# Eight k-tile pairs of each down stage in seven block products, three of them with differences formed by an accumulating transfer

## The chip, the cores and the metric

The kernel runs on one core of a Trainium2 chip. The metric is the device time in microseconds of one execution. The engines are named as in the profile: PE is TensorE's matmul, PEld its weight load, DVE is VectorE, ACT is ScalarE, POOL is GpSimd, SP is the engine that issues most of the transfers.

## The reference

A decoder trunk of two layers over 256 tokens of width 1024. Layer A has differential attention with a causal mask, layer B attention in blocks (one block of 256 here) with keys and values of its own; both attend to a fixed memory of 256 rows as well. Each layer ends in a squared-ReLU block of width 4096, and this is the part that the change concerns:

```python
x = x + jnp.concatenate([o_self, o_mem], axis=-1) @ w_out
x = x + _sq_relu_mlp(_rmsnorm(x, norm_mlp), w_up, w_down)

def _sq_relu_mlp(h, w_up, w_down):
    u = jax.nn.relu(h @ w_up)
    return (u * u) @ w_down
```

All data are float32. The down product has 256 tokens, 4096 inner columns (32 k-tiles of 128) and 1024 outputs.

## The kernel before

**Products in three passes.** Each float32 operand is split into a high part (a copy that rounds to the type float32r) and a low part (the value less the high part), and a product is three matmuls: high by high, low by high, high by low. For weights, `chunk` loads a piece of [128, 1024] into one of four `w` buffers, ACT makes the high part in one of six `wh` buffers and DVE the low part in one of six `wl` buffers (line 364).

**Stages.** Mixer A (projections, attention, output projection), up A and down A (`mlp`), mixer B, up B and down B with the final norm (`mlp_last`). In an up stage `mlp_up` (from line 818) goes over 16 blocks of two column tiles, and leaves u squared as high and low parts in eight large buffers B0 to B7, four k-tiles in each. Each large buffer comes free once the products of its tiles are done.

**The down stages.** `natural_down` goes over the k-tiles, two at a time: a pair j is the k-tiles 2j and 2j + 1. Its product is a 2 by 2 block matter: u has the blocks (k-tile, half of the tokens), the weights the blocks (k-tile, half of the outputs). The ordinary way takes eight block products of three matmuls with 512 columns. For the pairs in the list `FAST`, `fast_pair` takes seven, by Winograd's form of Strassen's method. It needs four sums and differences of the u blocks, formed in the up stage by `block_sums`, and four of the weight blocks. With W00, W01 the halves of the first tile and W10, W11 those of the second, `diff` forms on DVE (line 963), in the room's blocks 0 to 3 of 512 columns each: W01 - W00, then W11 less that, W11 - W01, and W10 less block 1. `split` (lines 955 and 956) makes high and low parts of the four kinds of weights: W00 alone, the second tile (1024 columns), the room's blocks 0 and 1, the room's blocks 2 and 3. So a fast pair takes four of the six `wh` and four of the six `wl` buffers. The sums of u are split at lines 982 and 983. The seven products go to four cells of the result and to four further banks, which `gather` joins when the last fast pair is done.

Before, `FAST` is one list for both layers, and the room is one buffer, `near`, which all fast pairs share; it also serves one chunk of the up stage.

In down A the pairs 0 to 11 go through `natural_down`, and the last eight k-tiles follow by halves of the outputs. In down B all 32 k-tiles do, and the products of the last six k-tiles are put at the end, cell by cell, among the final norm's steps.

**The order.** Nothing is issued in the order of the code. `Plan.add` records each step with the engine, an estimated duration, what it reads and writes, and a priority (its place in the code less a shift). `Plan.order` then simulates the engines and picks at each moment the step that is ready and has the lowest priority; buffers of the classes in `fifo` are handed out in the order in which the code names them. The shifts, one for each kind of step and layer, are the table `EARLY`. The engines work in the order so found, each in order: an instruction that waits holds up all behind it. Loads go out on SP's queue alone.

Of the kernel before, what the change touches and what calls it, by code (L numbers as in the profile page):

```python
# [14 lines left out]
OP = mybir.AluOpType  # L15
# [9 lines left out]
HELD = 6  # L25
FAST = (0, 2, 4, 6, 8, 9, 11)
CW = 1024
LEAD = 16
MN = 7
SUMS = -10  # L30
# [8 lines left out]
EARLY = {k + l: 0 for k in KINDS for l in "AB"}  # L39
EARLY.update(wA=40, wB=-21, memA=20, memB=31, natA=25, natB=64, statA=-80, statB=-115, ropeA=-90, ropeB=9, scoreA=-92,  # L40
             scoreB=-37, ptA=136, ptB=-40, pvA=-41, pvB=145, finA=158, finB=85, evacA=55, evacB=167, prepA=154,
             prepB=60, normA=120, normB=36)
LOOK = 100
# [22 lines left out]
class Plan:  # L66
# [3 lines left out]
    LAT = 200  # L70
    SAME = {"pe": 0, "act": 130, "dve": 130, "pool": 130, "dma": 0}

# [52 lines left out]
    def order(self):  # L125
        look = {"pe": 0, "act": LOOK, "dve": LOOK, "pool": 0, "dma": 0}
        ready = {e: [] for e in self.SAME}
# [105 lines left out]
def tile_hybrid(ctx: ExitStack, tc: tile.TileContext, x0, xa, xb, xc, memt, xnat, mnat, w0, wall, consts, fgain, out):  # L233
# [8 lines left out]
    for i in range(8):  # L242
        caps[f"B{i}"] = 1
    P = Plan(caps, ("acc", "w", "wh", "wl", "v") + tuple(f"B{i}" for i in range(8)))
    uid = [0]
# [5 lines left out]
    def buf(cls, shape, dt=F32, pool=None):  # L251
        pool = pool or ring
        return Buf(cls, lambda slot: pool.tile(shape, dt, name=name(cls), tag=f"{cls}{slot}", bufs=1))
# [75 lines left out]
    def dma(dst, src, nbytes, r=(), w=(), pri=None, rate=0, lag=1900):  # L329
        rate = rate or 340  # L330
        P.add(("dma", max(470, nbytes / rate), lambda: nc.sync.dma_start(dst(), src)), r, w, lag=lag, pri=pri)

# [554 lines left out]

    def block_sums():

        sums = {}  # L890
        for i, j in enumerate(FAST):
            if i < 2:
                b = ppx_buf()
                dst, keys = (lambda b=b: b.t), [b]
            elif i < 5:
                dst = lambda i=i: vb.rearrange("p a b e -> p (a b e)")[:, (i - 2) * 512:(i - 1) * 512]
                keys = [("vb", n, hf) for n in range(2) for hf in range(2)]
            elif i == 5:
                dst, keys = (lambda: mv.rearrange("p a b e -> p (a b e)")), [("mv", 0), ("mv", 1)]
            else:  # L900
                n = ("mk", "qm")[i - 6]
                dst, keys = (lambda n=n: {"mk": mkr, "qm": qmr}[n]), [(n, 0), (n, 1)]
            sums[j] = dst, keys + [("s", j)]
        st_["sums"] = sums
        return sums

    def sums_room():

        room = buf("near", [128, 2048])
        return lambda a, b: room.t[:, a:b], lambda a: [(room, a)]  # L910

    def natural_down(us, pss, upto, held, gather, room, rk, depth):

# [3 lines left out]


        cells = list(pss)
        more = [bank("acc") for _ in range(4)]  # L920
# [22 lines left out]
        def fast_pair(n, j):  # L943

            i = st_["i"]
            st_["i"] += 2
            w = [buf("w", [128, CW]) for _ in range(2)]
            h = [buf("wh", [128, CW], F32R) for _ in range(4)]
            l = [buf("wl", [128, CW], F32R) for _ in range(4)]
            for a in range(2):  # L950
                dma(lambda a=a: w[a].t, wall[i + a], 4 * 128 * CW, w=[(w[a], 0), (w[a], 1)])
            old, P.shift = P.shift, EARLY["w" + st_["layer"]]

# [11 lines left out]
            def wb(a, c):  # L965
                return lambda: w[a].t[:, c * 512:c * 512 + 512]
            wk = [(x, c) for x in w for c in range(2)]
            split(0, wb(0, 0), [wk[0]], 512)
            diff(0, wb(0, 1), wb(0, 0), wk[:2])
            split(1, lambda: w[1].t, wk[2:])  # L970
            diff(1, wb(1, 1), lambda: t(0), [wk[3]] + rk(0))
            split(2, lambda: t(0, 2), rk(0) + rk(1))
            diff(2, wb(1, 1), wb(0, 1), [wk[1], wk[3]])
            diff(3, wb(1, 0), lambda: t(1), [wk[2]] + rk(1))
# [17 lines left out]
            k0, k1 = ukeys(us, 2 * j), ukeys(us, 2 * j + 1)  # L992
            end = n == len(FAST) - 1
            for ps, a, ak, x, c, last in (
# [7 lines left out]
        for k in range(upto):  # L1002
            if k // 2 in FAST:
                ch.append(None)
                if k % 2:
                    fast_pair(FAST.index(k // 2), k // 2)
                continue
            ch.append(chunk())
            if k < held:
                for hf, c in cells:  # L1010
                    mm(k, hf, c)
        return mm, product, u_

    def mlp(st, done):
        us = mlp_up(st, block_sums())
        pss = {(hf, c): bank("t") for c in range(2) for hf in range(2)}
        ys = {(hf, c): buf("q" + "hl"[c], [128, 512]) for hf, c in pss}

        def gather(more):
# [10 lines left out]
            for (hf, c), y in ys.items():  # L1030
                P.add(("act", t_act(512, False, True), lambda y=y, hf=hf: nc.scalar.activation(
                    y.t, y.t, AF.Copy, scale=st.r[:, hf:hf + 1])), [y, st.key], [y])

        part = 24
        _, product, u_ = natural_down(us, pss, part, part, gather,
                                      *sums_room(), 4)
        for c in range(2):
# [26 lines left out]
    def mlp_last(st):  # L1064
# [8 lines left out]
        for hf, c in cells:  # L1073
# [9 lines left out]
            xs[hf, c] = x  # L1083
        us = mlp_up(st, block_sums())
        pss = {cell: bank("t") for cell in cells}
# [24 lines left out]
        held = 32 - HELD  # L1110
        mm = natural_down(us, pss, 32, held, gather, *sums_room(), 4)[0]
        x, ps, tail = xs[1, 1], pss[1, 1], bank("acc")
# [372 lines left out]
```

## Time and profile before

| | |
|---|---|
| median of three runs | 589.21 us (588.25 to 590.46) |
| profiled execution | 589.23 us |
| its span, first to last instruction | 587.3 us |
| DVE differences of line 963 (three groups of 28, 14 and 14) | 19.2, 9.6 and 9.6 us |
| bytes moved by transfers | 107.38 MB, mean 183 GB/s |

The profile is that of one execution. Its page gives the busy time of each engine, the costliest groups of instructions with the idle time before them, and the transfers. Views of the trace give more: the order of time of one engine, the busy time of each engine in any stretch of the span, and who waited for whom. A matmul's row is longer than the time from its start to the next one's start, since matmuls are pipelined; so is a DVE row, by a little. Costs are therefore read from start to start. A time in brackets at the end of a row is idle time of the engine ahead of it, with what ended it.

### The profile page before, as it was taken

Reading aid. Unit: us, or ns where it says so; the run is one execution under the profiler, and the core shown is the slowest. Engines: PE = TensorE matmul, PEld = TensorE weight load, DVE = VectorE, ACT = ScalarE, POOL = GpSimd, SP = SyncE. Lnnn points to the kernel's source line nnn. Section 1 sums busy time; section 2 is a strip of 40 time slices with the busy share of each in tenths; the row PEclk is TensorE's granted clock in tenths of the full one; section 3 lists DMA queues with packets and bytes.
Section 4 is the critical chain, followed back from the end, with each engine's and each line's share of the span. In section 5 each row is a group of like instructions: output and inputs, shape, how many; then the busy total and the mean of one; then the engine's idle time right before and its main releaser. Section 6 shows DMA issues by size and latency. Waiting matters only on the chain.

```text
span 587.3 us, 10340 instructions
## 1 busy us (share of the span) xinstructions
PE 577.8 (98%) x3786; PEld 511.1 (87%) x3786; DVE 480.5 (82%) x838; ACT 410.7 (70%) x787; POOL 63.8 (11%) x74
## 2 busy tenths in 40 slices
PE   8999999999999999999999999999999999999995
PEld 7787778999999988888888887889999999888884
DVE  6798998787676889998988688797866677998985
ACT  6677988677667676576776588776776676656632
POOL 0422030240000000000112222001300000000002
PEclk9999999999999999999999999999999999999999
DMA  8666456447655545657577633324755564555521
GB/s 284 210 227 219 155 171 225 133 155 219 200 193 191 169 145 197 234 169 251 174 244 239 205 121 124 126 75 143 247 192 205 182 185 139 194 201 210 193 98 72
DMA packets 30866, 107.38 MB, mean 183 GB/s; under 512 B 3424, under 2 KB 3680, under 8 KB 30816
## 3 DMA queue, kind: packets, MB, share of 16 engines
q1 hardware_dynamic: 30528, 106.21, 54.3%
q8 instruction: 29, 0.48, 0.3%
q10 hardware_dynamic: 288, 0.52, 0.2%
q14 instruction: 21, 0.17, 0.1%
HBM read 105.67 MB, written 1.05 MB: 182 GB/s over the span
## 4 chain that ended last, share of the span: by engine, by line
PE 90%; DMA 4%; ACT 2%; DVE 2%; issue 1%; SPq 0%; POOL 0%; DVEq 0%; ACTq 0%; POOLq 0%
PE acc L864 30%; PE t L932 19%; PE acc L523 17%; PE acc L804 8%; PE acc L932 7%; PE t L623 2%; PE t L661 2%; DMA w<-memt 2%; PE t L718 1%; PE t L594 1%; ACT wh L362 1%; DMA w<-wall 1%; DVE wl L364 1%; DMA xT<-xb 1%; PE t L523 1%
## 5 line engine op out<-in xcount | busy, mean ns | idle before, releaser
L364 DVE TENSOR_TENSOR wl<-w,wh 128x512 fp32r<-128x512 f32 (+1 forms) x226 | 209.8, 951 | 45.4 <-ACT wh L362 44.3
L362 ACT CAST wh<-w 128x512 fp32r<-128x512 f32 (+1 forms) x227 | 177.3, 812 | 90.3 <-PE acc L864 41.2
L864 PE MATMUL acc<-xn,wh 128*128 128x256 f32 x1024 | 127.6, 277 | 0.0
L864 PEld LDWEIGHTS acc<-xn,wh 128*128 128x128 f32 x1024 | 121.5, 188 | 0.0
L932 PE MATMUL t<-wh,B 128*128 128x512 f32 (+1 forms) x344 | 104.6, 386 | 0.0
L932 PEld LDWEIGHTS t<-wh,B 128*128 128x128 f32 x344 | 64.2, 188 | 13.1
L523 PE MATMUL acc<-wh,xn 128*128 128x512 f32 x220 | 72.9, 398 | 0.5 <-ACT wh L362 0.5
L864 PE MATMUL acc<-xn,wl 128*128 128x256 f32 x496 | 66.5, 276 | 0.0
L932 PE MATMUL t<-wl,B 128*128 128x512 f32 (+1 forms) x172 | 66.3, 386 | 0.0
L864 PEld LDWEIGHTS acc<-xn,wl 128*128 128x128 f32 x496 | 61.0, 188 | 0.0
L482 POOL TENSOR_TENSOR sqa<-sqa,sq 128x256 f32<-128x256 f32 x28 | 27.0, 963 | 250.7 <-ACT sq L481 247.8
L523 PEld LDWEIGHTS acc<-wh,xn 128*128 128x128 f32 x220 | 41.3, 188 | 11.2 <-issue 1.8
L804 PE MATMUL acc<-B,wh 128*128 128x256 f32 x256 | 50.0, 287 | 0.0
L523 PE MATMUL acc<-wl,xn 128*128 128x512 f32 x110 | 43.1, 392 | 0.3 <-DVE wl L364 0.2
L804 PEld LDWEIGHTS acc<-B,wh 128*128 128x128 f32 x256 | 40.7, 189 | 0.6 <-issue 0.5
L955 ACT CAST wh<-near 128x1024 fp32r<-128x1024 f32 x28 | 29.3, 1054 | 13.4 <-DVE near L963 6.5
L932 PEld LDWEIGHTS t<-wl,B 128*128 128x128 f32 x172 | 32.3, 188 | 6.6 <-DVE wl L364 0.2
L955 ACT CAST wh<-w 128x512 fp32r<-128x512 f32 (+1 forms) x28 | 23.4, 835 | 18.2 <-PE t L932 12.2
L804 PE MATMUL acc<-B,wl 128*128 128x256 f32 x128 | 35.7, 279 | 0.0
L956 DVE TENSOR_TENSOR wl<-near,wh 128x1024 fp32r<-128x1024 f32 x28 | 33.9, 1223 | 1.9 <-ACT wh L955 0.5
L570 POOL TENSOR_TENSOR ropet<-ropes,consts 128x256 f32<-128x256 f32 (+1 forms) x28 | 26.0, 950 | 76.2 <-ACT ropes L559 58.6
L956 DVE TENSOR_TENSOR wl<-w,wh 128x512 fp32r<-128x512 f32 (+1 forms) x28 | 26.4, 954 | 7.1 <-ACT wh L955 7.1
(238 smaller groups left out, 906.5 us busy)
## 6 DMA issues: line engine op xcount, KB each, us to landing
w<-wall SPq DMA_DIRECT2D x188, 512.0 KB, 3.9
w<-memt SPq DMA_DIRECT2D x4, 512.0 KB, 5.2
w<-wall SPq DMA_DIRECT2D x6, 256.0 KB, 5.0
B<-mnat SPq DMA_DIRECT2D x2, 512.0 KB, 7.2
w<-w SPq DMA_DIRECT2D x2, 256.0 KB, 3.5
xT<-xc SPq DMA_DIRECT2D x2, 256.0 KB, 5.5
consts<-consts SPq DMA_DIRECT2D x1, 256.5 KB, 6.0
xT<-xb SPq DMA_DIRECT2D x1, 256.0 KB, 4.6
```

Source lines behind the costliest of these rows:

```text
L362: P.add(("act", t_act(n), lambda sl=sl: nc.scalar.copy(h.t[:, sl], w.t[:, sl])), [(w, x) for x in q], [(h, x) for x in q])
L364: P.add(("dve", t_dve(n), lambda sl=sl: nc.vector.tensor_sub(l.t[:, sl], w.t[:, sl], h.t[:, sl].bitcast(F32))), [(w, x) for x in q] + [(h, ...
L482: P.add(("pool", t_pool(S), lambda: nc.gpsimd.tensor_tensor(self.acc.t, self.acc.t, sq.t, op=OP.add)), [sq, self.acc], [self.acc])
L523: nc.tensor.matmul(pss[hf].t[:, c0:c1], a(k)[:, ts], b.t[:, o + c0:o + c1], start=(k == 0 and i == 0), stop=(k == KT - 1 and i == 2))
L570: nc.gpsimd.tensor_tensor(t.t[:, 0:nh, e:e + 32], zs.t[:, 0:nh, 32 - e:64 - e], b(sin[:, e:e + 32]), op=OP.mult)
L623: nc.tensor.matmul(sp[hd].t[:, c], qk[a].t[r, qb * 128:(qb + 1) * 128], qk[b].t[r, S:S + c.stop - c.start], start=(qb == 0 and i == 0 and ...
L661: nc.tensor.transpose(ps.t[:, i * 128:(i + 1) * 128], p.t[:, j * 128:(j + 1) * 128], ident)
L804: nc.tensor.matmul(o, a.t[:, ws], x(k), start=(n == 0 and m % 2 == 0 and i == 0), stop=(n == KT - 1 and i == 2), skip_group_check=True)
L864: nc.tensor.matmul(ps.t[:, o], w.t[:, k * 128:(k + 1) * 128], xnt[:, k, x], skip_group_check=True, **flags)
L932: nc.tensor.matmul(ps.t[:, c0:c1], x, y, start=start and i == 0, stop=stop and i == 2, skip_group_check=True)
L955: P.add(("act", t_act(m), lambda: nc.scalar.copy(h[x].t[:, :m], src())), keys, [h[x]])
L956: P.add(("dve", t_dve(m), lambda: nc.vector.tensor_sub(l[x].t[:, :m], src(), h[x].t[:, :m].bitcast(F32))), keys + [h[x]], [l[x]], port=True)
```

## The change

The list of fast pairs becomes one for each layer, with eight pairs instead of seven. For three of them (`ADDED`: numbers 0 and 5 of A's list, pairs 0 and 9, and number 6 of B's list, pair 11) blocks 0 and 2 of the room, W01 - W00 and W11 - W01, aren't formed on DVE. A transfer loads the first weight tile into them, ACT negates them, and a transfer issued by POOL adds the second halves of both tiles. The room of each fast pair is named in `ROOMS`: -1 is `near`, a number is that large buffer. `near` joins the classes handed out in order, the planner has a new engine for the accumulating transfers (1000 ns, and 4700 ns until they land), and the table `EARLY` has new numbers.

```diff
-FAST = (0, 2, 4, 6, 8, 9, 11)
+FAST = {"A": (0, 2, 4, 6, 7, 9, 10, 11), "B": (0, 2, 4, 6, 7, 10, 11, 12)}
+ADDED = {"A": (0, 5), "B": (6,)}
+ROOMS = {"A": (-1, -1, -1, 0, 0, -1, 2, -1), "B": (-1, -1, -1, -1, -1, 3, 2, 0)}
...
-EARLY.update(wA=40, wB=-21, memA=20, memB=31, natA=25, natB=64, statA=-80, statB=-115, ropeA=-90, ropeB=9, scoreA=-92,
-             scoreB=-37, ptA=136, ptB=-40, pvA=-41, pvB=145, finA=158, finB=85, evacA=55, evacB=167, prepA=154,
-             prepB=60, normA=120, normB=36)
+EARLY.update(wA=31, wB=-10, memA=20, memB=42, natA=10, natB=64, statA=-98, statB=-92, ropeA=-110, ropeB=35, scoreA=-92,
+             scoreB=-26, ptA=117, ptB=-20, pvA=-17, pvB=118, finA=175, finB=153, evacA=86, evacB=204, prepA=211,
+             prepB=34, normA=110, normB=14)
...
-    P = Plan(caps, ("acc", "w", "wh", "wl", "v") + tuple(f"B{i}" for i in range(8)))
+    P = Plan(caps, ("acc", "w", "wh", "wl", "v", "near") + tuple(f"B{i}" for i in range(8)))
...
-    def sums_room():
+    def sums_room(layer):
-        room = buf("near", [128, 2048])
-        return lambda a, b: room.t[:, a:b], lambda a: [(room, a)]
+        near = buf("near", [128, 2048])
+        which = []
+        rooms = {-1: (lambda a, b: near.t[:, a:b], lambda a: [(near, a)])}
+        for i in ROOMS[layer]:
+            if i not in rooms:
+                r = big(i, [128, 2048])
+                rooms[i] = (lambda a, b, r=r: r.t[:, a:b], lambda a, r=r: [(r, a)])
+            which.append(rooms[i])
+        return which
...
         def fast_pair(n, j):
+            room, rk = rooms[n]
...
-            for a in range(2):
-                dma(lambda a=a: w[a].t, wall[i + a], 4 * 128 * CW, w=[(w[a], 0), (w[a], 1)])
...
+            added = n in ADDED[layer]
+            if added:
+                def both():
+                    return room(0, 2048).rearrange("p (a b n) -> p a b n", a=2, b=2)[:, :, 0]
+                bk = rk(0) + rk(2)
+                dma(both, wall[i].rearrange("p (a n) -> p a n", a=2), 4 * 128 * CW, w=bk)
+                P.add(("act", t_act(CW), lambda: nc.scalar.mul(both(), both(), -1.0)), bk, bk)
+                P.add(("sw", 1000, lambda: nc.gpsimd.dma_start(
+                    both(), wall[i:i + 2, :, 512:1024].rearrange("a p n -> p a n"), accum_op=OP.add)), bk, bk, lag=4700)
+            for a in range(2):
+                m = 512 if added and not a else CW
+                dma(lambda a=a, m=m: w[a].t[:, 0:m], wall[i + a, :, 0:m], 512 * m, w=[(w[a], 0), (w[a], 1)])
...
-            diff(0, wb(0, 1), wb(0, 0), wk[:2])
+            if not added:
+                diff(0, wb(0, 1), wb(0, 0), wk[:2])
             split(1, lambda: w[1].t, wk[2:])
             diff(1, wb(1, 1), lambda: t(0), [wk[3]] + rk(0))
             split(2, lambda: t(0, 2), rk(0) + rk(1))
-            diff(2, wb(1, 1), wb(0, 1), [wk[1], wk[3]])
+            if not added:
+                diff(2, wb(1, 1), wb(0, 1), [wk[1], wk[3]])
```

More of the change, by code (lines that the diff above doesn't have):

```diff
@@ L70 @@
     LAT = 200
-    SAME = {"pe": 0, "act": 130, "dve": 130, "pool": 130, "dma": 0}
+    SAME = {"pe": 0, "act": 130, "dve": 130, "pool": 130, "dma": 0, "sw": 0}
     def __init__(self, caps, fifo):
@@ L125, in order @@
     def order(self):
-        look = {"pe": 0, "act": LOOK, "dve": LOOK, "pool": 0, "dma": 0}
+        look = {"pe": 0, "act": LOOK, "dve": LOOK, "pool": 0, "dma": 0, "sw": 0}
         ready = {e: [] for e in self.SAME}
@@ L886, in up_chunk, with block_sums @@
                   [("xnh", j) for j in range(k, k + 4)] + [(wl, k // 4)], [ps] + [between] * bool(between))
-    def block_sums():
+    def block_sums(layer):
         sums = {}
-        for i, j in enumerate(FAST):
+        for i, j in enumerate(FAST[layer]):
             if i < 2:
@@ L905, in block_sums, with natural_down @@
         return sums
-    def sums_room():
-        room = buf("near", [128, 2048])
-        return lambda a, b: room.t[:, a:b], lambda a: [(room, a)]
-    def natural_down(us, pss, upto, held, gather, room, rk, depth):
+    def sums_room(layer):
[8 more added lines that the diff above has]
+        return which
+    def natural_down(layer, us, pss, upto, held, gather, rooms, depth):
+        fast = FAST[layer]
         cells = list(pss)
@@ L949, in fast_pair @@
             l = [buf("wl", [128, CW], F32R) for _ in range(4)]
-            for a in range(2):
-                dma(lambda a=a: w[a].t, wall[i + a], 4 * 128 * CW, w=[(w[a], 0), (w[a], 1)])
-            old, P.shift = P.shift, EARLY["w" + st_["layer"]]
             def split(x, src, keys, m=CW):
@@ L967, in fast_pair @@
             wk = [(x, c) for x in w for c in range(2)]
+            added = n in ADDED[layer]
[10 more added lines that the diff above has]
+                dma(lambda a=a, m=m: w[a].t[:, 0:m], wall[i + a, :, 0:m], 512 * m, w=[(w[a], 0), (w[a], 1)])
+            old, P.shift = P.shift, EARLY["w" + st_["layer"]]
             split(0, wb(0, 0), [wk[0]], 512)
-            diff(0, wb(0, 1), wb(0, 0), wk[:2])
+            if not added:
+                diff(0, wb(0, 1), wb(0, 0), wk[:2])
             split(1, lambda: w[1].t, wk[2:])
@@ L992, in fast_pair @@
             k0, k1 = ukeys(us, 2 * j), ukeys(us, 2 * j + 1)
-            end = n == len(FAST) - 1
+            end = n == len(fast) - 1
             for ps, a, ak, x, c, last in (
@@ L1002, in natural_down @@
         for k in range(upto):
-            if k // 2 in FAST:
+            if k // 2 in fast:
                 ch.append(None)
                 if k % 2:
-                    fast_pair(FAST.index(k // 2), k // 2)
+                    fast_pair(fast.index(k // 2), k // 2)
                 continue
@@ L1014, in mlp @@
     def mlp(st, done):
-        us = mlp_up(st, block_sums())
+        us = mlp_up(st, block_sums("A"))
         pss = {(hf, c): bank("t") for c in range(2) for hf in range(2)}
@@ L1034, in mlp @@
         part = 24
-        _, product, u_ = natural_down(us, pss, part, part, gather,
-                                      *sums_room(), 4)
+        _, product, u_ = natural_down("A", us, pss, part, part, gather, sums_room("A"), 4)
         for c in range(2):
@@ L1083, in mlp_last @@
             xs[hf, c] = x
-        us = mlp_up(st, block_sums())
+        us = mlp_up(st, block_sums("B"))
         pss = {cell: bank("t") for cell in cells}
@@ L1110, in mlp_last @@
         held = 32 - HELD
-        mm = natural_down(us, pss, 32, held, gather, *sums_room(), 4)[0]
+        mm = natural_down("B", us, pss, 32, held, gather, sums_room("B"), 4)[0]
         x, ps, tail = xs[1, 1], pss[1, 1], bank("acc")
```

## The prediction

> **What bounds the kernel now.** I read the head of the page first, then the table of busy time by stretches (which I cut where the lines of the kernel change), then the order of time of single engines inside the down stages, then the waits.
>
> ```profile
> span 587.3 us, 10340 instructions
> ...
> PE 577.8 (98%) x3786; PEld 511.1 (87%) x3786; DVE 480.5 (82%) x838; ACT 410.7 (70%) x787; POOL 63.8 (11%) x74
> ```
>
> TensorE is busy for all but 587.3 - 577.8 = 9.5 us. The table by stretches says where those 9.5 us are. Its columns: stretch, its length, then busy time and count of PE, weight loads, DVE, ACT, POOL, the granted clock, the DMA share, GB/s. The stretches are head, mixer A, up A, down A (three), mixer B and its projection (two), up B, down B (two), tail.
>
> ```profile
> 0.00:25.00 25.00, 22.72 (x114) 18.03 (x115) 17.09 (x34) 17.00 (x36) 6.75 (x12) 1.00 0.83 269
> 25.00:122.00 97.00, 96.81 (x627) 81.41 (x627) 86.02 (x208) 77.91 (x221) 18.53 (x19) 1.00 0.54 184
> 122.00:209.90 87.90, 87.90 (x774) 87.86 (x773) 64.18 (x91) 62.60 (x89) 6.58 (x7) 1.00 0.56 181
> 209.90:254.90 45.00, 45.00 (x199) 37.25 (x200) 41.96 (x51) 29.32 (x35) 0.00 (x0) 1.00 0.59 202
> 254.90:266.50 11.60, 11.60 (x53) 9.61 (x52) 11.60 (x14) 7.71 (x10) 0.00 (x0) 1.00 0.60 209
> 266.50:292.20 25.70, 25.60 (x117) 21.00 (x116) 23.04 (x38) 20.13 (x38) 2.69 (x3) 1.00 0.60 205
> 292.20:398.20 106.00, 106.00 (x659) 87.61 (x658) 89.07 (x192) 76.82 (x192) 16.82 (x20) 1.00 0.50 164
> ...
> 497.70:557.60 59.90, 59.90 (x265) 49.58 (x266) 56.45 (x67) 39.70 (x47) 0.00 (x0) 1.00 0.58 203
> 557.60:580.40 22.80, 22.77 (x118) 19.29 (x116) 16.84 (x34) 8.08 (x19) 5.03 (x7) 1.00 0.25 89
> 580.40:587.30 6.90, 0.00 (x0) 0.00 (x0) 2.82 (x11) 1.12 (x3) 0.00 (x0) 0.86 0.20 76
> ```
>
> Two things are to be seen. First, the idle time of TensorE is 2.28 us of head, 6.90 us of tail and a few tenths between: every stage is bound by TensorE, the down stages too, at a granted clock of 1.00. Second, DVE is the runner-up, and in the down stages a close one: in down A up to 266.5 it is busy for 41.96 + 11.60 = 53.56 of 56.60 us (3.04 idle), in down B up to 557.6 for 56.45 of 59.90 (3.45 idle). In the up stage it has 87.90 - 64.18 = 23.72 us to spare.
>
> **The gain: products that go.** A k-tile pair done the ordinary way is eight block products, a fast pair seven; each product is three 512-column matmuls. One product, in the order of time on TensorE:
>
> ```profile
> 213.27 0.62 PE L932 MATMUL acc<-wh,xn 128*128 128x512 f32 x2
> 213.72 0.39 PE L932 MATMUL acc<-wl,xn 128*128 128x512 f32 x1
> 213.95 0.62 PE L932 MATMUL acc<-wh,xn 128*128 128x512 f32 x2
> ```
>
> From start to start that is 213.95 - 213.27 = 0.68 us, 0.227 us a matmul (the 0.39 us of one row overlaps the next). An ordinary pair is 8 x 0.68 = 5.44 us, a fast one 7 x 0.68 = 4.76. The lists go from seven to eight fast pairs in each layer, so two products, six matmuls, leave: 2 x 0.68 = 1.36 us. Nothing is added on TensorE. This is the whole gain, 0.23%.
>
> **The price on DVE.** The step to step times of DVE come from its order of time:
>
> ```profile
> 225.72 0.68 DVE L963 TENSOR_TENSOR near<-w,near 128x512 f32<-128x512 f32 x1
> 226.32 1.29 DVE L983 TENSOR_TENSOR xn<-vb,xn 128x512 fp32r<-128x512 f32 x2
> 227.59 1.23 DVE L956 TENSOR_TENSOR wl<-near,wh 128x1024 fp32r<-128x1024 f32 x1
> 228.74 1.22 DVE L364 TENSOR_TENSOR wl<-w,wh 128x1024 fp32r<-128x1024 f32 x1
> 229.87 0.68 DVE L963 TENSOR_TENSOR near<-w 128x512 f32<-128x512 f32 x1
> ```
>
> A 512-wide step takes 226.32 - 225.72 = 0.60 us, a 1024-wide one 229.87 - 228.74 = 1.13, say 1.14. A fast pair has six of the narrow (four differences, the short split, the split of a block sum) and three of the wide: 3.60 + 3.42 = 7.02 us. An ordinary pair has two wide ones: 2.28. So a fast pair needs 7.02 us of DVE for 4.76 us of TensorE, an ordinary one 2.28 for 5.44; turn about they fit (9.30 in 10.20), in a row they don't. One more fast pair costs DVE 7.02 - 2.28 = 4.74 us in each layer. Where a transfer forms two of the differences, two narrow steps go: 1.20 us, twice in A (pairs 0 and 9), once in B (pair 11). Net: +2.34 us in A, +3.54 in B. The block sums of the eighth pair are four short DVE steps more in each up stage, which its 23.72 us hide.
>
> Is there room? In A, pair 0 is prepared before 209.9, where DVE has time anyhow, so of its 1.20 us nothing counts later. From 209.9 to 266.5: idle 3.04, less 4.74 - 1.20 = 3.54, less 0.68 by which TensorE is sooner: 1.18 us short. In B up to 557.6: 3.45 - 3.54 - 0.68 = 0.77 short. These are the upper bounds of a new stall, 1.95 us. Lower bound nothing, for two reasons. What idle time DVE has there is not lack of work ahead but full buffers:
>
> ```profile
> 251.73 1.23 DVE L956 TENSOR_TENSOR wl<-w,wh 128x1024 fp32r<-128x1024 f32 x1 [1.04 <-ACT wh L955]
> ```
>
> DVE waits for ACT's split. The next row, from ACT's order of time, shows that ACT had waited for a product to release the buffer:
>
> ```profile
> 250.64 1.05 ACT L955 CAST wh<-w 128x1024 fp32r<-128x1024 f32 x1 [2.05 <-PE t L932]
> ```
>
> The change gives the differences of pairs 6, 7 and 10 in layer A and of 10, 11 and 12 in layer B other rooms than the one that all share now (buffers whose u tiles have been used), so DVE can form them in such gaps instead of waiting for the one room. And in B the last fast pair is now pair 12, after which come three ordinary pairs; behind 557.6 DVE has 22.80 - 16.84 = 5.96 us to spare. I take nothing, since TensorE's record has no gap in these stages (45.00 of 45.00, 59.90 of 59.90) with pairs 8 and 9 already side by side, and keep 1.95 for the range.
>
> **ACT, POOL and the queues.** A fast pair has five splits on ACT instead of two, and each of the three transfers brings a negation of 1024 elements, by the row below about 1.05 us; ACT has 45.00 - 29.32 = 15.68 us to spare in the first stretch of down A alone, so nothing counts.
>
> ```profile
> L955 ACT CAST wh<-near 128x1024 fp32r<-128x1024 f32 x28 | 29.3, 1054 | 13.4 <-DVE near L963 6.5 <-PE acc L864 3.2 <-PE acc L932 2.5
> ...
> w<-wall SPq DMA_DIRECT2D x188, 512.0 KB, 3.9
> ...
> B<-mnat SPq DMA_DIRECT2D x2, 512.0 KB, 7.2
> ```
>
> (The last two rows: size of one, median us to landing.) Each added pair loads 512 KB into the room, loads 256 KB less into the first w buffer and adds 512 KB by an accumulating transfer from POOL: 0.77 MB, three times 2.3 MB of 107. With a DMA share of 0.59 there is room. The room's load is issued on SP's queue, in order: if the room isn't free, the weight loads behind it wait too. The rooms are long free by the plan (near since pair 4, B2 since pair 5), so I take nothing.
>
> The accumulating transfer itself is in no row of this trace. Bounds: 3.9 us, if it goes like a load, and 3 x 3.9 = 11.7, if it reads its target, writes it and runs alone at a third of the pace; 7.2 is the longest landing shown for its size. The plan reserves 1.0 + 4.7 = 5.7 us. I take about that: between 3.9 and 7.2 it costs nothing, because the chain (load 3.9, negation 1.05, transfer) can start whole pairs ahead.
>
> POOL and DVE are seen to slow each other:
>
> ```profile
> L482 POOL TENSOR_TENSOR sqa<-sqa,sq 128x256 f32<-128x256 f32 x28 | 27.0, 963 | 250.7 <-ACT sq L481 247.8
> ...
> L1151 POOL TENSOR_TENSOR ql<-ql,ropes 128x256 f32<-128x256 f32 x2 | 1.4, 737 | 2.7 <-ACT sq L1140 2.7
> ```
>
> The same sum of 128x256 takes 963 ns in the up stages and mixers, beside a busy DVE, and 737 behind 557.6, where DVE has idle time. A transfer that POOL issues might be held up likewise, by 963 / 737 = 1.3 times: 0.3 us on the plan's 1.0, which the lead hides. The Trainium skill, SBUF — State Buffer, "Who interferes with whom", speaks against such transfers from POOL: its descriptors need a port that DVE's two-port modes lock; it adds that a sum of two tensors takes only the read side and so should not stop them. By the first half the three transfers would be held as long as DVE is in such a mode, by the second not at all; nearly all of DVE's steps in the down stages are such sums, so the sum above stands either way. No row here shows descriptor writing beside DVE.
>
> **The retuned leads.** They reorder work in every stage, the mixers above all. What can be won: in 25.0 to 122.0 TensorE is idle for 0.19 us, in 292.2 to 398.2 for none, in the head 2.28. With the 0.1 of down A that is at most 2.6 us, and part of the head is the first load, which no lead shortens. What can be lost has no such bound in the trace; DVE's 86.02 of 97.00 and 89.07 of 106.00 say that a late rope or turn can be made up for only in part.
>
> ```profile
> PE acc L523 <- ACT wh L362: 0.5, 1, 0.5
> ```
>
> That is TensorE's longest wait for a split of weights (total, times, longest, in us). I take zero, from -2.6 to +3; the 3 is an estimate, six waits of that length.
>
> **Sum.** Against the profiled execution, 589.23 us with a span of 587.3 (1.93 us lie around it; the median of the three runs is 589.21, the same within 0.02): 589.23 - 1.36 = 587.87. **587.9 us.**
>
> **Rivals.**
> 1. DVE takes over in the down stages. For it: 7.02 against 4.76 us for a fast pair, three of them in a row (9, 10, 11 in A; 10, 11, 12 in B), six wl buffers of which a pair takes four. Against it: the rooms and the ordinary pairs behind. At the full 1.95 us: 589.8; at half 588.9.
> 2. The leads gain as well: 587.87 - 2.6 = 585.3 at best; about 586.3 if a good half of it comes.
> 3. Slower: the accumulating transfers land late. The place is the difference of block 1 in pairs 9 (A) and 11 (B), a DVE step that needs the sum. DVE works in order, so behind it stand the splits of the same pair and of the next ones, and TensorE waits for those. It decides from where the lateness passes what DVE can make up, about its 3 us of idle. At 11.7 us instead of the plan's 5.7 it is 6.0 late, less 3.0, in two places: 6.0 us, 593.9. Pair 0 is sheltered by the up stage. For it: no row bounds that transfer, and DVE is nearly full. Against it: the room is free whole pairs ahead. The page DMA: Bandwidth & Descriptors of the Trainium skill, "Anatomy of one DMA", fits 2.0 us + bytes / 436 GB/s for plain transfers of this kind; as an estimate that is 3.2 us for 512 KB, which would leave the sum as it is.
> 4. The leads open gaps in the mixers: up to +3, 590.9.
> 5. The change does less than it says, because TensorE was not the bound there: excluded as to counts (six matmuls go), and the full stretches leave little doubt that each is worth its 0.227 us.
>
> **How the numbers follow.** Forecast with small deviations (587.2 to 588.6): 0.52. Rival 1 (588.6 to 589.8): 0.18. Rival 2: 0.10. Rival 3: 0.11. Rival 4: 0.09. A half per cent, about what a measurement of this kernel tells from no change, is 2.95 us: faster is below 586.3, slower above 592.2. Faster: most of rival 2, 0.08. Slower: most of rival 3 and the end of rival 4 joined with 1, 0.12. Same: 0.80. The range reaches from 585.8 to 591.5: below it lies a third of rival 2, above it rival 3 and little else, some 0.15 in all.
>
> **What would show it.** Right: the matmul rows of line 932's successor number 738 instead of 744, TensorE's busy time falls by about 1.4 us, stretches of the down stages stay full, DVE is busy near 100% there. Rival 1: weight loads or matmuls in the down stages that wait for DVE's wl splits, a few tenths each, in pairs 7 and 10 to 12. Rival 3: a DVE step idle for microseconds with a DMA into near or B2 as its releaser. Rivals 2 and 4: the head's or the mixers' idle time of TensorE changes while the down stages do what they should. The prediction is wrong if the down stages save something other than 0.68 us each, or if the mixers move by more than the saving.

## The result, and the profile after

The changed kernel takes 592.32 us (median of seven runs), the kernel before 588.78 in the same job. One of the seven took 642.93 us at a granted clock of 0.85; without it the median is 592.0, slower by 3.3 us, and the ratio is 1.0058 [1.0045, 1.0071]. Run again in another job (e16) it took 591.62 against 588.88, 1.0043 [1.0028, 1.0059]. The forecast was 587.9 with a range up to 591.5.

The page of the changed kernel (its profiled execution took 593.29 us, the longest of the other six): its span, the counts, and the rows of the transfers that are new (size of one, median us from issue to landing).

```profile
span 591.2 us, 10374 instructions
...
PE 578.3 (98%) x3780; PEld 509.7 (86%) x3780; DVE 486.5 (82%) x852; ACT 417.6 (71%) x798; POOL 66.7 (11%) x77
...
near<-wall POOLq DMA_DIRECT2D x2, 512.0 KB, 9.5
B<-wall POOLq DMA_DIRECT2D x1, 512.0 KB, 7.8
```

Six matmuls are gone, 3786 to 3780, yet TensorE's busy time rose from 577.8 to 578.3 and its idle time from 9.5 to 591.2 - 578.3 = 12.9 us. Why the busy time rose the runs do not show. The adding transfers land 9.5 (median of 8.3 and 10.6) and 7.8 us after their issue; the plan had 5.7. TensorE's waits (total, times, longest) name what is new beside the 1.1 us at the start that both kernels have:

```profile
PE t L596 <- ACT B L742: 1.3, 1, 1.3
PE acc L525 <- DVE wl L366: 1.2, 3, 0.8
...
PE acc L525 <- ACT wh L364: 0.5, 1, 0.5
PE t L596 <- ACT o L764: 0.5, 1, 0.5
PE t L942 <- DVE xn L1006: 0.5, 1, 0.5
```

L596 lies in mixer A, L525 in the products of the mixers (the wait of 0.8 at the hand-over from down A to mixer B), L942 is the down stage. None was there before but those of L525, with 0.2 and 0.5. The wait of 1.3 was 0.4 in e15 and none of 0.2 or more in e16, which have the same mixer A, so it isn't a steady cost.

One measure served through all runs: the **length of layer B's block**, from the first matmul of up B to the last of down B, read from TensorE's order of time. The ends for the kernel before,

```profile
408.61 0.48 PE L864 MATMUL acc<-xn,wh 128*128 128x256 f32 x2
...
580.09 0.28 PE L932 MATMUL acc<-wl,B 128*128 128x256 f32 x1
```

and for the changed one:

```profile
411.84 0.48 PE L866 MATMUL acc<-xn,wh 128*128 128x256 f32 x2
...
583.79 0.28 PE L942 MATMUL acc<-wl,B 128*128 128x256 f32 x1
```

That is 171.5 before and 172.0 after: longer by 0.5, though one product fewer should make it 0.7 shorter. The same reading from the first matmul of down A to the first of up B, called the **middle** below, gives 198.8 and 200.4. Both are read from one execution of each kernel. B's block repeats to 0.1 us between kernels with the same number of pairs in B and no adding transfer in it. The middle doesn't: it is 198.5 to 199.1 in the kernel before and e5, e6, e8, e10, e11 and e12, which have seven pairs in A and not the new table, so differences of up to 0.6 us in it tell little.

### The profile page after: what moved, and what is told of

It reads as the page before. It is cut to its first block, busy times and chain, and to the rows that moved or that the text cites. A ratio compares the mean times of both kernels' runs of the same rounds, so it can differ in the third digit from the quotient of the medians.

```text
span 591.2 us, 10374 instructions
## 1 busy us (share of the span) xinstructions
PE 578.3 (98%) x3780; PEld 509.7 (86%) x3780; DVE 486.5 (82%) x852; ACT 417.6 (71%) x798; POOL 66.7 (11%) x77
## 4 chain that ended last, share of the span: by engine, by line
PE 88%; ACT 4%; DMA 3%; DVE 3%; issue 1%; SPq 0%; DVEq 0%; ACTq 0%
PE acc L866 30%; PE t L942 19%; PE acc L525 14%; PE acc L942 8%; PE acc L806 8%; PE t L625 3%; DMA w<-wall 2%; ACT wh L364 2%; PE t L720 1%; PE t L663 1%; DVE wl L366 1%; PE t L525 1%; DMA w<-memt 1%; PE t L596 1%; SPq L333 0%
## 5 line engine op out<-in xcount | busy, mean ns | idle before, releaser
L942 PE MATMUL t<-wh,B 128*128 128x512 f32 (+1 forms) x320 | 97.1, 385 | 0.0
L525 PE MATMUL acc<-wh,xn 128*128 128x512 f32 x220 | 73.5, 399 | 0.7 <-ACT wh L364 0.5
L942 PEld LDWEIGHTS t<-wh,B 128*128 128x128 f32 x320 | 59.7, 188 | 12.1
L942 PE MATMUL t<-wl,B 128*128 128x512 f32 (+1 forms) x160 | 61.7, 386 | 0.1
L525 PEld LDWEIGHTS acc<-wh,xn 128*128 128x128 f32 x220 | 41.3, 188 | 12.3 <-issue 2.1
L525 PE MATMUL acc<-wl,xn 128*128 128x512 f32 x110 | 43.2, 393 | 0.5 <-DVE wl L366 0.5
L942 PEld LDWEIGHTS t<-wl,B 128*128 128x128 f32 x160 | 30.0, 188 | 6.6 <-DVE wl L964 0.6
L572 POOL TENSOR_TENSOR ropet<-ropes,consts 128x256 f32<-128x256 f32 (+1 forms) x28 | 24.2, 885 | 69.3 <-ACT ropes L561 56.3
L644 ACT ACTIVATE B<-t,small 128x128 f32<-128x128 f32 (+1 forms) x64 | 27.1, 439 | 4.1 <-DVE small L636 3.1
L942 PE MATMUL acc<-wh,xn 128*128 128x512 f32 x96 | 29.5, 389 | 0.0
```

Source lines behind the costliest of these rows:

```text
L525: nc.tensor.matmul(pss[hf].t[:, c0:c1], a(k)[:, ts], b.t[:, o + c0:o + c1], start=(k == 0 and i == 0), stop=(k == KT - 1 and i == 2))
L572: nc.gpsimd.tensor_tensor(t.t[:, 0:nh, e:e + 32], zs.t[:, 0:nh, 32 - e:64 - e], b(sin[:, e:e + 32]), op=OP.mult)
L644: nc.scalar.activation(p[hd].t[:, c], sp[hd].t[:, c], AF.Exp, bias=nm[hd][:, qb:qb + 1], accum_out=ss[:, hd, qb:qb + 1])
L942: nc.tensor.matmul(ps.t[:, c0:c1], x, y, start=start and i == 0, stop=stop and i == 2, skip_group_check=True)
```

## The experiments

All times are medians, beside the kernel before in the same job. The ratios with their 95% intervals are worked out from the single runs and aren't the quotients of the two medians (e8: 0.9986 by the medians, 0.9999 in the table, with one run of 592.27 us among its twelve). "Old leads" and "new leads" are the two tables `EARLY` of the diff.

### Which half of the change costs: e1 to e4

e1 is the kernel before with the new leads; e2 the changed kernel with the old leads; e3 the changed kernel without transfers of differences; e4 the changed kernel with two leads taken back.

```diff
# e1: before              EARLY.update(new numbers)
# e2: changed             EARLY.update(old numbers)
# e3: changed
-ADDED = {"A": (0, 5), "B": (6,)}
+ADDED = {"A": (), "B": ()}
# e4: changed
-EARLY.update(wA=31, ... natA=10,
+EARLY.update(wA=40, ... natA=25,
```

> The kernel before with the new table of leads alone (seven pairs, no added transfers). Theory L (most of the loss is the new leads: they put a weight load between the two loads of mnat, and tighten the start of mixer B): the first matmul of up A comes about 1.7 us later than before, that of up B about 3.6 us later, down stages as before; time about 592.0, ratio 1.0055. Rival T (the loss is the eighth pairs with their transfers): 588.7, ratio 1.000.

> The changed kernel with the old table of leads (eight pairs, transfers, rooms). Theory L: up A and up B start as in the kernel before; the down stages give back 1.36 us of products and lose about 1.3 us to late weight loads beside the transfers: 588.8 plus or minus 0.7, ratio 1.000. Rival T: 591.5 or more, ratio 1.005.

> The changed kernel with all differences on DVE (eight pairs, rooms, new leads, no transfers). Theory A (the transfers delay the weight loads beside them): the stall of about 1.1 us near the end of down B goes, the one in down A stays or grows to 1.3 us because DVE has 2.4 us more to do there; against the changed kernel between -1.0 and +0.5: 591.3 to 592.8. Rival D (DVE is the bound in the down stages, and the transfers relieve it): both down stages stall by 1 to 2 us more: 594 or more.

> The changed kernel with two leads put back, wA=40 and natA=25, after which the loads of mnat go out one behind the other as before. Theory L: the wait of about 1.8 us in mixer A (at 58 us) goes, up A starts 1.7 us sooner, mixer B keeps its loss: 590.6, ratio 1.003. If the mnat loads do not matter: 592.3.

| | us | before | ratio | B's block | middle |
|---|---|---|---|---|---|
| e1 | 590.47 | 588.87 | 1.0029 [1.0020, 1.0039] | 171.5 | 200.1 |
| e2 | 590.14 | 588.87 | 1.0020 [1.0002, 1.0038] | 172.2 | 199.4 |
| e3 | 590.80 | 588.87 | 1.0036 [1.0022, 1.0049] | 170.8 | 201.7 |
| e4 | 591.00 | 588.87 | 1.0036 [1.0024, 1.0048] | 172.3 | 199.5 |

Both halves cost, where theory L and rival T each named one: e1 is 1.5 us below the 592.0 of theory L, e2 1.3 above its 588.8. The new leads alone make the kernel before 1.6 us slower. The pairs with the old leads are 1.3 slower, where 1.36 faster was worked out. Without transfers B's block falls to 170.8, by just the 0.7 that a product less is worth. The total is 1.9 us above the kernel before, where the changed kernel is 2.7 (e16) to 3.3 above it. The middle grew to 201.7 in its profiled execution (592.67 us, the longest of its eight runs), and TensorE has a new wait in down A, at 269.2 us:

```profile
PE t L942 <- DVE xn L1006: 0.9, 1, 0.9
```

With this list, and without transfers, DVE is late in layer A by 0.85 us. (L1006 is DVE's split of a sum of u.) The changed kernel, e15 and e16 have the same list with the transfers of pairs 0 and 9, and no wait in down A: there the transfers did relieve DVE. Two leads taken back (e4) change little against e16's 1.0043.

### The eighth pair by layer: e5 to e8

All with the old leads. e5 has seven pairs in A, and in B the eight of the change with their rooms but no transfer; e6 is e5 with pair 11's transfer; e7 has the change's eight pairs, rooms and two transfers in A, and the old seven in B; e8 has seven in both, and pair 11 of B formed by the transfer in a large buffer.

```diff
# e5: changed, old leads
+FAST = {"A": (0, 2, 4, 6, 8, 9, 11), "B": (0, 2, 4, 6, 7, 10, 11, 12)}
+ADDED = {"A": (), "B": ()}
# e6: e5 with             ADDED = {"A": (), "B": (6,)}
# e7: changed, old leads
+FAST = {"A": (0, 2, 4, 6, 7, 9, 10, 11), "B": (0, 2, 4, 6, 8, 9, 11)}
+ADDED = {"A": (0, 5), "B": ()}
# e8: changed, old leads
+FAST = {"A": (0, 2, 4, 6, 8, 9, 11), "B": (0, 2, 4, 6, 8, 9, 11)}
+ADDED = {"A": (), "B": (6,)}
```

> Eight pairs in layer B alone, all differences on DVE, old leads, the rooms of B as in the change; layer A as in the kernel before. Theory A (the late weight loads beside the transfer cost down B its gain): without the transfer the gain of 0.68 us stands, nothing waits near the end of down B: 588.2 against 588.9, ratio 0.999. Rival D (DVE is short there, by 0.77 us plus the 1.20 us that the transfer took off it): a stall of 1 to 2 us in pairs 10 to 12, 589.5 or more.

> As e5, but pair 11's two differences by the transfer as in the change. Theory A: ACT and DVE wait 2 to 4 us for the weight loads beside the transfer, TensorE about 1.2 us near 556 us: 589.4, 1.2 us more than e5. Rival D: faster than e5, because DVE has 1.20 us less to do.

> Eight pairs in layer A alone, with its two transfers, old leads; layer B as in the kernel before. Theory E (the last splits of down A come later, so the loads of the memory for mixer B and its first weights start later against TensorE): down A gains 0.68 less 0.44, then TensorE waits about 1.0 us near the start of mixer B; up B starts about 0.8 us later than before: 589.6. Without such a hand-over: 588.4.

> The kernel before with one thing more: the two differences of pair 11 of layer B by the transfer (seven pairs, old leads). Theory A: DVE has 1.20 us less to do and yet the weight loads beside the transfer land late, ACT waits for them 3 us or more; TensorE stalls by 0 to 1 us: 588.9 to 589.9. If the transfer cost nothing: 588.9 and no wait of ACT for weights over 2 us in down B.

| | us | before | ratio | B's block | middle |
|---|---|---|---|---|---|
| e5 | 587.72 | 588.70 | 0.9987 [0.9976, 0.9998] | 170.8 | 198.5 |
| e6 | 589.80 | 588.70 | 1.0031 [1.0019, 1.0044] | 172.3 | 199.0 |
| e7 | 588.42 | 588.70 | 0.9999 [0.9989, 1.0009] | 171.4 | 199.1 |
| e8 | 587.88 | 588.70 | 0.9999 [0.9983, 1.0014] | 171.5 | 198.7 |

e5 has the product's gain and nothing else. Its DVE and ACT, in the order of time where pair 11 is prepared (idle time before a row in brackets, with what ended it):

```profile
539.40 1.05 ACT L963 CAST wh<-w 128x1024 fp32r<-128x1024 f32 x1 [1.58 <-DMA w<-wall]
...
539.47 0.69 DVE L971 TENSOR_TENSOR B<-w,B 128x512 f32<-128x512 f32 x1 [0.15 <-DMA w<-wall]
```

The same two steps in e6, with the transfer:

```profile
541.47 1.06 ACT L963 CAST wh<-w 128x1024 fp32r<-128x1024 f32 x1 [3.69 <-DMA w<-wall]
...
541.54 0.69 DVE L971 TENSOR_TENSOR B<-w,B 128x512 f32<-128x512 f32 x1 [2.44 <-DMA w<-wall]
```

Both engines start 2 us later (2.7, counted from the first matmul of up B, at 408.05 us in e5 and 407.41 in e6), and the releaser is not the sum that the transfer forms, which landed at 540.53: it is `w`, an ordinary weight load on SP's queue, issued at 534.71 and landed at 541.45. In the changed kernel the same step of DVE waits 2.19 us for `w<-wall`. What that does further on is in the table by stretches (length, then busy time and count of PE, weight loads, DVE, ACT, POOL), of e5 first:

```profile
545.00:556.00 11.00, 11.00 (x50) 9.13 (x49) 11.00 (x15) 7.23 (x9) 0.00 (x0) 1.00 0.54 179
```

and of e6:

```profile
545.00:556.00 11.00, 10.08 (x44) 7.74 (x43) 10.96 (x16) 7.78 (x9) 0.00 (x0) 1.00 0.50 162
```

DVE is full in both. In e5 it keeps TensorE fed for 11.00 of 11.00 us; in e6, with the later start, it doesn't make up the time, and TensorE does 44 matmuls instead of 50. (The two stretches are shifted by 0.64 us against each other; B's block, 170.8 and 172.3, is not.) e8 has a transfer for pair 11 too, but only seven fast pairs, and TensorE has no wait in the stage:

```profile
545.00:556.00 11.00, 11.00 (x50) 9.12 (x49) 9.41 (x11) 7.62 (x9) 0.00 (x0) 1.00 0.65 222
```

DVE has 1.59 us of 11 left there. But e8 differs in a second way: its transfer lands at 539.93, over 5 us before DVE's first use of the sum at 545.36, and neither ACT nor DVE waits for a load between 530 and 552. So that a late load costs only where DVE has no idle time left is argued from these three runs, not shown.

### What of the transfer is late: e10 and e11

e10 is e6 with a plain transfer of the same bytes in place of the adding one, so that the addition is left out; e11 is e6 with pair 0 instead of pair 11 formed by a transfer, in the up stage.

```diff
# e10: e6 with
-    both(), wall[i:i + 2, :, 512:1024].rearrange("a p n -> p a n"), accum_op=OP.add)), bk, bk, lag=4700)
+    both(), wall[i:i + 2, :, 512:1024].rearrange("a p n -> p a n"))), bk, bk, lag=4700)
# e11: e6 with            ADDED = {"A": (), "B": (0,)}
```

> As e6, but the transfer of POOL's queue writes the second halves instead of adding them (so the differences of pair 11 are wrong in value; same bytes, same waits, same queue). Theory P (an adding packet holds an engine twice as long, 197 against some 95 ns, and so the weight loads behind it come late): its packets take about 95 ns, ACT waits under 2.5 us for the weight load instead of 3.7, TensorE does not stall: 588.0, near e5. Rival Q (the queue itself is the cost: whatever POOL issues goes ahead of SP's loads): 589.8, as e6.

> As e6, but the transfer serves pair 0 instead of pair 11, so it runs in the up stage, where DVE is idle for a quarter of the time. Theory A: weight loads beside it may be late, but DVE makes it up: 587.8, as e5. Rival R (a transfer of POOL costs its 2 us wherever it stands): 589.8.

e10: 587.95, before 588.74, 0.9990 [0.9979, 1.0001], B's block 170.8. e11: 588.09, 0.9989 [0.9979, 0.9999], B's block 170.8. Neither has the 1.5 us of e6's 172.3. In e11 the transfer lands even later after its issue (7.7 us in e6), and TensorE has no wait in layer B's block:

```profile
near<-wall POOLq DMA_DIRECT2D x1, 512.0 KB, 8.3
```

So it is the adding, at that place. e10 tells how much lateness is too much. The same step of ACT there:

```profile
540.86 1.05 ACT L963 CAST wh<-w 128x1024 fp32r<-128x1024 f32 x1 [2.89 <-DMA w<-wall]
```

Counted from up B's first matmul (408.21) that is 1.3 us later than in e5, where e6 is 2.7 later. DVE is as full as in e6 (10.96 of 11.00 us from 545 to 556), and TensorE doesn't wait: 1.3 us are still made up for, 2.7 are not. The 2.89 us are more than the 2.5 that the expectation allowed.

The single packets in the trace show where the time goes. Here they are counted by the microsecond in which they start, with their bytes and mean duration (SP's counts hold the packets of 4 B that end a load, 14 of the 27 in 536 in e6):

```
                    packets of POOL's queue            SP's queue, us 535 536 537 538 539 540
e6  adding   256 of 2048 B, 194 ns, 536.2 to 539.8                 59  27   0   6  81 173
e10 plain    128 of 4096 B, 193 ns, 536.4 to 538.9                 69  66   0  48 125 161
```

For the same 512 KB the adding transfer needs twice the packets, each half as large but taking the same time: 256 x 194 / 16 = 3.1 us on all sixteen DMA engines, against 128 x 193 / 16 = 1.5. (The expectation had it that the plain packets would be as many and half as long; the total is the same.) And while either is served, SP's queue all but stops (33 packets from 536 to 539 in e6, 114 in e10; in the changed kernel one from 541 to 543). The Trainium skill, Collectives: The Full Stack, "The bandwidth ceiling: the fold count and why AG ≠ RS ≠ AR", says of ReduceScatter, a collective whose transfers add, that it is slower because the add needs two source reads, which makes its rate about half. The trace agrees with the half (3.1 against 1.5 us).

The Trainium skill, DMA: Bandwidth & Descriptors, "Queues, rings and completion order", says that a DMA engine goes round robin between its queues, but drains a whole packet, typically 9 to 17 descriptors, from one before it switches. Its packet is not a packet of the profile. The profile counts these on POOL's queue, in e6 and in e10:

```profile
q0 software_dynamic: 272, 0.52, 0.5%
...
q0 software_dynamic: 144, 0.52, 0.3%
```

Spread evenly over sixteen engines these are 17 and 9 for each, with the one of 4 B that ends its share. If each share goes as one packet of the skill's kind, SP's loads stand still for the whole transfer, and the trace agrees with that: in 537 they had none in either run, though in e6 one had been issued at 534.71. Where such a packet ends the profile doesn't show, so this cause of the standstill is argued; the standstill is shown.

### The eighth pair of A without transfers, and two leads: e9 and e12

e9 has eight pairs in both layers, no transfers, old leads, and another list in A; e12 is the kernel before with two of the new leads.

```diff
# e9: e5 with
+FAST = {"A": (0, 1, 3, 5, 6, 8, 10, 11), "B": (0, 2, 4, 6, 7, 10, 11, 12)}
+ROOMS = {"A": (-1, -1, -1, -1, -1, 0, -1, -1), "B": (-1, -1, -1, -1, -1, 3, 2, 0)}
# e12: before
-EARLY.update(wA=40, ... natA=25,
+EARLY.update(wA=31, ... natA=10,
```

> Eight pairs in both layers with all differences on DVE: layer B as in e5, layer A with the list 0, 1, 3, 5, 6, 8, 10, 11 and one second room, old leads. Theory A (the gain was lost to the transfers and the leads, not to DVE): both stages shorter by 0.7 us, 587.5 to 588.0 against 588.8, ratio 0.998; a hand-over to mixer B that is late (theory E) takes up to 0.7 us of it back. Rival D (DVE cannot carry eight pairs): 590 or more.

> The kernel before with two leads of the new table, wA=31 and natA=10, which put a weight load between the two loads of mnat and move the rest of mixer A's order. Theory L: these two are most of what the new leads cost: 590.1, ratio 1.0022; a wait of TensorE for ACT at 58 us. If the other leads cost it (mixer B): 588.8.

e9: 588.45, before 588.74, 0.9992 [0.9981, 1.0004], B's block 170.8, middle 199.8. e12: 588.63, 1.0004 [0.9993, 1.0015]. The pair of B gains its 0.7 again; that of A gains nothing, without transfers too, and TensorE has no wait in down A: with this list DVE carries eight pairs. The two leads are harmless alone.

### The leads by layer, the transfer alone, the change again: e13 to e16

e13 and e14 are the kernel before with the new leads of layer A's names only, and of layer B's only; e15 is the changed kernel without pair 11's transfer (`ADDED["B"] = ()`); e16 is the changed kernel.

```diff
# e13: before             EARLY.update(all ...A names new, ...B names old)
# e14: before             EARLY.update(all ...B names new, ...A names old)
# e15: changed
-ADDED = {"A": (0, 5), "B": (6,)}
+ADDED = {"A": (0, 5), "B": ()}
```

> The kernel before with the new leads of layer A only. The new table cost 1.7 us, two of its entries (wA, natA) nothing. Theory LA (the order of mixer A as a whole, with the split pair of mnat loads, is the cost): 590.2. Theory LB (the order of mixer B is the cost): 588.8.

> The kernel before with the new leads of layer B only. Theory LA: 588.8. Theory LB: 590.2, up B starts about 1 us later against up A than before.

> The changed kernel, all of it, less the one transfer of pair 11 in layer B. Theory A: the 2.1 us that this transfer cost in e6 against e5 come back here too: 590.2, no stall near 559 us. If the losses are not additive: 591.5 or more.

> The changed kernel once more, beside e15: 592.3, ratio 1.006. Its wait for ACT in mixer A at 58 us, 1.8 us in its first profile and 0.5 us in e1 with the same order of loads, is expected between those.

| | us | before | ratio | B's block | middle |
|---|---|---|---|---|---|
| e13 | 589.16 | 588.88 | 1.0006 [0.9996, 1.0016] | 171.5 | 199.4 |
| e14 | 589.37 | 588.88 | 1.0018 [0.9999, 1.0037] | 171.5 | 199.6 |
| e15 | 589.98 | 588.88 | 1.0023 [1.0011, 1.0034] | 170.8 | 199.7 |
| e16 | 591.62 | 588.88 | 1.0043 [1.0028, 1.0059] | 172.1 | 200.3 |

Pair 11's transfer costs the changed kernel 591.62 - 589.98 = 1.6 us. Neither theory LA nor LB came, since neither layer's numbers alone reach 590.2 us or e1's 1.0029; those of B come nearer, but with an interval that touches 1 (one of e14's runs took 595.47 us). TensorE's waits in e1 don't point to one place either:

```profile
PE acc L523 <- ACT wh L362: 1.0, 1, 1.0
PE t L1056 <- DVE qh L1047: 0.6, 1, 0.6
PE t L594 <- ACT o L762: 0.5, 1, 0.5
PE acc L523 <- DVE wl L364: 0.4, 2, 0.2
```

The first and the last are near the start, at 7 to 10 us, where the kernel before has 0.5 and 0.2; the L594 is in mixer A and the L1056 at the end of down A. The wait at L1056 stands in e13 too (0.7 us) and not in e14, so it comes of layer A's numbers. Layer B's show otherwise: from the last matmul of down A to the first of up B takes 114.8 us in e14 and e1, 114.1 in e13 and the kernel before, with the same matmuls. So both halves of the table have a part, in these traces 0.6 to 0.7 us each. That the new table costs 1.6 us is shown; which entries do it stays open.

### Where A's pair loses its gain: e17 and e18

In e7 ACT's order of time at the hand-over from down A to mixer B has this, and TensorE's the second row:

```profile
283.17 1.71 ACT L380 ACTIVATE wh<-w,xT 128x256 fp32r<-128x256 f32 x4 [1.63 <-DMA w<-memt]
...
292.71 0.50 PE L525 MATMUL acc<-wl,wh 128*128 128x512 f32 x1 [0.73 <-DVE wl L366]
```

ACT stands still for the second load of layer B's memory rows. Behind it in its order are the normed input and the first weight splits of mixer B, and TensorE waits 0.73 us for the low part of one of those, which DVE forms behind ACT. That wait is 0.4 to 1.1 us in the seven runs so far with eight pairs in A other than e15, which has none, and in the runs with seven no such wait stands there. The load is later by more than the 0.68 us that the stage is shorter: counted from the first matmul of down A, it is issued after 65.6 us in all ten kernels with seven pairs in A and after 68.3 to 69.6 in all ten with eight. Why it is issued later the runs don't show. e17 and e18 are e9 and e7 with one edit: the planner expects layer B's memory loads 1.6 us later, and so gives ACT other work first.

```diff
-            dma(lambda w=w: w.t, memt[:, 4 * a:4 * a + 4], 4 * 128 * CW, w=[w])
+            dma(lambda w=w: w.t, memt[:, 4 * a:4 * a + 4], 4 * 128 * CW, w=[w], lag=1900 + 1600 * (st_["layer"] == "B"))
```

> Eight pairs in A and in B, the old leads, no transfer of differences (as e9, 588.45 at 0.9992), and the planner is told that layer B's memory loads land 1.6 us later than it thought. Theory: the eighth pair of A gives back its 0.68 at the hand-over to mixer B, because the second memory load lands after the time at which ScalarE's in-order stream asks for it (waits of 1.3 to 1.6 us there in the changed kernel and in e7); with the later due time ScalarE does the work behind it first, the 0.6 to 0.8 us wait of PE for the weight split near 293 us goes, the stretch from the first matmul of down A to the first of up B falls from 199.8 to about 199.1, and the time is about 587.8 (ratio 0.998). Rival: the memory load is only where the wait shows, something later is as late; the stretch stays at 199.4 to 199.8 and the time at 588.4.

> As e7 (eight pairs and their transfers in A, seven in B, old leads: 588.42 at 0.9999) with the same later due time of layer B's memory loads. Theory: the wait of 0.73 us of PE for the weight split at 293 us goes, down A to up B falls from 199.1 to about 198.4, time about 587.8 (0.9989). Rival: no change, 588.4.

e17: 587.34, before 588.76, 0.9970 [0.9957, 0.9982], middle 197.8. e18: 587.67, 0.9981 [0.9969, 0.9993], middle 197.8. In e17 ACT takes the normed input where it waited for the memory rows, and takes those later without a wait:

```profile
283.14 1.71 ACT L380 ACTIVATE xn<-xT 128x256 fp32r<-128x256 f32 x4 [0.80 <-DVE xT L790]
```

The largest of TensorE's waits in e17, apart from the one at the start, is:

```profile
PE acc L525 <- DVE wl L366: 0.4, 2, 0.2
```

The wait at the hand-over is gone, and the theory holds. The middle fell by 2.1 us from e9 and 1.3 from e7, more than the 0.7 expected. Part of that is a second wait of e9, 0.92 us at 307 us for ACT's `mv`, which is gone as well. Against the 198.5 to 199.1 with seven pairs, 197.8 is 0.7 to 1.3 shorter, where one product is worth 0.68. What the later due time would do with seven pairs wasn't tried, so how much of e17's gain is the pairs' is not shown. e17 is the fastest kernel of the study: the eight pairs of both layers, without transfers and without the new leads.

## Why the prediction was wrong, step by step

The prediction's own last sentence names two signs of being wrong, and both came: layer B's block saved nothing in the changed kernel (172.0 against 171.5), and the middle moved by more than the saving (200.4 against 198.8).

**The gain: right.** By the sum "two products, six matmuls, leave: 2 x 0.68 = 1.36 us". The count is 3780, and B's block shrinks by 0.7 us to 170.8 in every run with eight pairs in B and no adding transfer in pair 11 (e3, e5, e9, e10, e11, e15 and e17, against 171.4 to 171.5 with seven).

**The price on DVE: right for the changed kernel.** "I take nothing" of the 1.95 us of rival 1. In layer B, e5 forms all eight pairs' differences on DVE, 1.20 us more work than in the case that the sum has as 0.77 us short; DVE is then full, and TensorE doesn't wait. In layer A the changed kernel has no wait in down A either, but e3, without the transfers, has one of 0.85. So rival 1 falls in B, and in A it depends on the transfers or on the list (e9). But that fullness removed the reserve that the next step counted on.

**ACT, POOL and the queues: this step failed.** "With a DMA share of 0.59 there is room", and, of the adding transfer, "between 3.9 and 7.2 it costs nothing". A mean share says nothing of the 3.6 us in which one queue holds the sixteen engines. The landing, 7.8 and 9.5 us, was past the 7.2 and within the bounds of 3.9 to 11.7, but in layer B it isn't the sum that was waited for: the weight load beside it was, by 2 to 3 us, and with DVE full this cost 1.2 to 1.5 us of B's block (172.0 to 172.3 against 170.8) and 1.6 to 2.1 us of the total (e15 to e16, e5 to e6). The 3.2 us estimated from the page DMA: Bandwidth & Descriptors of the Trainium skill, "Anatomy of one DMA", hold neither for the adding kind nor, beside SP's loads, for the plain one, which landed after 5.8 us in e10. POOL's hold-up was small, as taken: its issue took 1.20 to 1.33 us, where the plan had 1.0, though the two rows from which that was worked out are not the same operation (line 482 adds, line 1151 multiplies). Which half of the rule in the Trainium skill, SBUF — State Buffer, "Who interferes with whom", holds here, no run tells apart.

**Rival 3: the right culprit, the wrong victim.** It named the adding transfer and pair 11, but put the wait at "a DVE step that needs the sum", to be seen by "a DMA into near or B2 as its releaser". The releaser was `w<-wall`. Its 6.0 us in two places were 1.6 in one. In pairs 0 and 9 of A no cost showed: at pair 9 neither ACT nor DVE waits for a load in e7 or in the changed kernel (236 to 262 us), and TensorE has no wait in up A or down A.

**The retuned leads: this step failed too.** "I take zero, from -2.6 to +3" was a point put at the middle of a range that the trace did not narrow. Alone they cost 1.6 us (e1). Rival 4, "the leads open gaps in the mixers", is right in kind for layer A's numbers; those of B lengthen the mixer by 0.7 us without a gap. The chances, 0.11 for rival 3 and 0.09 for rival 4, took the two as alternatives; both came, along with the hand-over.

**What no step had.** The hand-over from down A to mixer B. With eight pairs in A the second memory load of mixer B is issued some 3 us later against TensorE, and ACT, in order, passes that on. This gave back the 0.68 of A's pair (e7 at 0.9999), and e17 and e18 got it back.

**The sum.** From -1.36: leads +1.6, pair 11's transfer +1.6 (e15 to e16), the hand-over +0.7, together +2.5. e16 shows +2.7. That it comes out so near is partly luck: each term is a difference of medians, with 0.6 us or more of interval either way, and e15 stands at +1.1 without a wait at the hand-over. The first job's +3.3 is 0.5 more than e16's, and its profile has the 1.3 us wait in mixer A that e16's has not in that size; this isn't explained further.

## What to carry to other kernels

Before moving work from a full engine to a transfer, look at what other loads are in flight in the microseconds that it occupies, not at the mean share: the queue beside it may stop, and the load that is late is then one that nobody changed. When a stage is reordered or gets shorter, see when the next stage's first loads are issued now, and which in-order engine asks for them. Take a retuned table of priorities apart from the edit that it came with, since each can hide the other's sign.

## What the hardware showed that was not expected

- An adding transfer of 512 KB went in 256 packets of 2048 B at 194 ns; the plain one of the same bytes in 128 of 4096 B at 193 ns. So it occupied the DMA engines for twice the time, 3.1 against 1.5 us.
- While POOL's transfer was served, SP's queue moved 0 to 6 packets in a microsecond, against 59 and 173 around it, for the plain transfer (1 us of none) as for the adding one (2 us of nearly none).
- In layer B's down stage seven fast pairs with the transfer (e8) and eight without (e5) are both free of waits; both together (e6) stall TensorE. With eight, a weight load 1.3 us late (e10) was made up for, one 2.7 us late (e6) was not.
